# Two of sixteen MLP units by plain products, and their right-hand sums formed later

## The chip, the cores and the metric

The kernel runs on one core of one Trainium2 chip. The metric is device time in microseconds (us) of one execution. Engines are named as the profile names them: PE (TensorE, matmul) with its weight loads PEld, DVE (VectorE), ACT (ScalarE), POOL (GpSimd) and SP, whose queue issues the loads from HBM.

## What is computed

A decoder trunk of two layers on x of 512 tokens by 1024 features, in float32. Each layer is a token mixer, a cross-attention into 256 memory tokens, and an MLP; a norm closes the trunk. The part that matters here:

```
h = h + o.reshape(b, s, 1024) @ w_o                       # end of the cross-attention
n = rmsnorm(h, mlp_norm)                                  # h * rsqrt(mean(h*h) + eps) * gain
h = h + square(relu(n @ w_up)) @ w_down                   # w_up 1024 x 4096, w_down 4096 x 1024
```

The norm's factor per token is not applied to n: h times the gain goes into the matmuls, and the factor's square is multiplied in behind the down projection, since relu and square let it pass (tile Rt).

## The kernel before

Activations lie transposed: hT holds 8 blocks of 128 features by 512 tokens. Float32 accuracy comes from splitting every operand into a rounded high part and a low rest (`hi_lo`: ACT writes the high part, L156 or, with a scale, L159; DVE subtracts it for the low part, L157 or L160), and every product is three matmuls, high by high, high by low, low by high (`mm3`, L177 to L179). Weights are tiles of 128 x 1024: a DMA into a raw tile (tag wr, 2 buffers), then wh and wl (3 buffers each). `chunk` does this for a plain projection, which is 24 matmuls of 512 columns (`proj`).

**The end of the cross-attention** is eight such projections `wo`, one for each block e of hT in the order 0, 4, 1, 5, 2, 6, 3, 7. Behind each, `after_o` adds the result to hT (`add_h`, L474, DVE) and prepares the MLP's right operands; `st.add` squares the block on ACT (L258) and adds it to the tile ssq on POOL (L270).

**The MLP** has four quarters (`qd`). A quarter computes 8 blocks of hidden features, as four units, and then eight plain down projections. A unit (class `Unit`) is a 2 x 2 block scheme with seven products in the place of eight (Winograd's form of Strassen's scheme): its left operands are four quarters of a weight block and four sums of them (A11, A12, A22, S1 to S4), formed by four additions on POOL in `load` (L968); its right operands are 256 columns wide. A product is 12 matmuls of 256 columns, a unit 84. The unit's weights are three raw tiles of 1024 columns (d1, d2, d3) and one of 512 (e, tag ptl).

Right operands: `Right` holds, for a pair of blocks j and j + 4, the quarters B11, B12 (block j, its halves of the tokens), B21, B22 (block j + 4), and T1 = B11 - B12, T2, T3 and Z. Each of B11, T1, B21, B22, T2, T3, Z is split high and low. `first` forms B11 and T1 behind the first block of a pair (the scaled copy at L930, the difference at L932), `second` the others behind the second block (L938 to L943). They stand in the tiles hgh and hgl (B11 with T1, B21 with B22), qkh and qkl (T3, T2) and pth (Z). All four pairs are needed by the first product `0.p1`, since each product sums over the four pairs.

The order of the products in a quarter is a string of names (unit.product) in `mlp`; the tile framework turns program order and priorities into one instruction order per engine, and each engine takes its instructions in that order. `load` and `weight` run at raised priority. In the first quarter `st0.rstd()` (8 matmuls of 2 columns, L292, then L295 on DVE and a power on POOL, L298) stands behind the eighth product and the spread of r2 (L308, Rt) behind the fourteenth.

Of the kernel before, what the change touches and what calls it, by code (L numbers as in the profile page):

```python
# [10 lines left out]
F32R = mybir.dt.float32r  # L11
# [7 lines left out]
D = 1024  # L19
# [17 lines left out]
def build(ctx, tc, a):  # L37
# [125 lines left out]
    def chunk(src):  # L163

        cnt[0] += 1
        i = cnt[0]
        started.append(i)
        with tc.high_priority(100 if len(started) > 4 else 0):
            raw = wp.tile([128, 1024], F32, tag="wr", name=f"wr_{i}", bufs=2)
            h = wp.tile([128, 1024], F32R, tag="wh", name=f"wh_{i}", bufs=3)  # L170
            lo = wp.tile([128, 1024], F32R, tag="wl", name=f"wl_{i}", bufs=3)
            SY.dma_start(out=raw, in_=src)
            hi_lo(h, lo, raw)
        return h, lo

# [721 lines left out]
        return os_, out_steps(3)  # L897

# [8 lines left out]
    class Right:  # L907


        def __init__(self, j, gname, gi):  # L910
            self.j, self.gname, self.gi, self.x = j, gname, gi, {}

        def __getitem__(self, name):
            return self.x[name]

        def tile(self, name):
            cnt[0] += 1
            return wk.tile([128, 1280], F32, tag="p", name=f"{name}_{cnt[0]}", bufs=2)

        def parts(self, names, src, tags):  # L920
            h, lo = t2k(tags[0], F32R), t2k(tags[1], F32R)
            hi_lo(h, lo, src)
            for i, n in enumerate(names):
                self.x[n] = (h[:, i * 256:(i + 1) * 256], lo[:, i * 256:(i + 1) * 256])

        def first(self):

            j = self.j
            self.B = self.tile("B")
            A.activation(out=self.B[:, :1024].rearrange("p (a c) -> p a c", a=4)[:, 0::2, :],  # L930
                         in_=hT[:, j, :].rearrange("p (a c) -> p a c", a=2), func=AF.Copy, scale=col(self.gname, self.gi + j))
            V.tensor_tensor(out=self.B[:, 256:512], in0=self.B[:, 0:256], in1=self.B[:, 512:768], op=ALU.subtract)  # L932
            self.parts(("B11", "T1"), self.B[:, :512], ("hgh", "hgl"))

        def second(self):
            j, B = self.j + 4, self.B
            E = self.tile("E")
            A.activation(out=E[:, :512], in_=hT[:, j, :], func=AF.Copy, scale=col(self.gname, self.gi + j))  # L938
            V.scalar_tensor_tensor(out=E[:, 768:1024], in0=B[:, 256:512], scalar=-1.0, in1=E[:, 256:512],
                                   op0=ALU.mult, op1=ALU.subtract)  # L940
            V.tensor_tensor(out=E[:, 512:768], in0=E[:, 256:512], in1=B[:, 512:768], op=ALU.subtract)
            self.parts(("B21", "B22"), E[:, :512], ("hgh", "hgl"))
            V.scalar_tensor_tensor(out=E[:, 1024:1280], in0=E[:, 768:1024], scalar=-1.0, in1=E[:, 0:256],  # L943
                                   op0=ALU.mult, op1=ALU.subtract)
            self.parts(("T3", "T2"), E[:, 512:1024], ("qkh", "qkl"))
# [84 lines left out]
    def mlp(li, xs, st0, gname, gi, st):  # L1030
        nhg = []

        end = gname is None

        def after_up(qd, i, hid):
            def fn(half, c):
                V.scalar_tensor_tensor(out=c, in0=c, scalar=0.0, in1=c, op0=ALU.max, op1=ALU.mult)
                if end and qd == 3:
                    V.tensor_tensor(out=c, in0=c, in1=Rt, op=ALU.mult)
                h, lo = t2k("acth", F32R), t2k("actl", F32R)  # L1040
                hi_lo(h, lo, c)
                hid[i + 4 * half] = (h, lo)
            return fn

        def after_down(qd, e):
            def fn(ps):
                if end and qd == 3:
                    add_h(e, ps)
                    st.add(e, hT[:, e, :])
                    A.activation(out=hT[:, e, :], in_=hT[:, e, :], func=AF.Copy, scale=col("final_norm", e))  # L1050
                    return
                t = t2k("kv")
                V.tensor_tensor(out=t, in0=ps, in1=Rt, op=ALU.mult)  # L1053
                V.tensor_tensor(out=hT[:, e, :], in0=hT[:, e, :], in1=t, op=ALU.add)
                if qd == 3:
                    new_h(e, gname, gi, nhg, st)
            return fn

        for qd in range(4):
            hid = {}  # L1060
            us = [Unit(a["mlp_up"][li * 16 + qd * 4 + i], xs, after_up(qd, i, hid)) for i in range(4)]
            if qd == 0:

                order = "0.p1 0.p5 1.p1 1.p5 0.p2 0.p6 1.p2 1.p6 0.p7 0.p4 0.p3"
            else:
                order = "0.p1 0.p5 0.p2 0.p6 1.p1 1.p5 0.p7 1.p2 1.p6 0.p4 0.p3"
            order += " 2.p1 2.p5 1.p7 2.p2 2.p6 1.p4 1.p3 3.p1 3.p5 2.p7 3.p2 3.p6 2.p4 2.p3"
            for i, x in enumerate(order.split()):
                getattr(us[int(x[0])], x[2:])()
                if qd == 0 and i == 7:  # L1070
                    st0.rstd()
                if qd == 0 and i == 13:
                    r2 = small(4, tag="r2")
                    V.tensor_tensor(out=r2, in0=st0.r, in1=st0.r, op=ALU.mult)
                    A.activation(out=Rt, in_=spread(r2), func=AF.Copy)
            prev = us[3]
            ks = (0, 4, 1, 5, 2, 6, 3, 7)
            down = [proj(a["mlp_down"][(li * 4 + qd) * 8 + e], hid, after_down(qd, e), ks=ks)
                    for e in range(7 if end and qd == 3 else 8)]
# [167 lines left out]
    for li in range(2):  # L1247
# [35 lines left out]
        wo = [proj(a["xa_w_o"][li * 8 + e], os_, after_o(i, e), need=need) for i, e in enumerate((0, 4, 1, 5, 2, 6, 3, 7))]
        merge(last, [*wo[0][:6], *wo[1][:6]])
        run([*wo[0][6:], *wo[1][6:]])
        for e in range(2, 8):
# [121 lines left out]
```

## Time and profile before

| | |
|---|---|
| runs, median of 3 | 1480.79 us (1480.47 to 1482.84) |
| the profiled execution | 1479.2 us, its span 1477.2 us |
| PE busy | 1425.7 us, 97% of the span |
| DVE, ACT, POOL busy | 1073.5, 747.2, 361.9 us |
| mean granted TensorE clock | 0.991 |
| line of PE over 40 slices | 7999999999899999999999999999998999999996 |

A matmul's record reaches past the start of the next one, because matmuls are pipelined; the time from one start to the next tells what one costs. A bracket at the end of a timeline row gives the idle time of the engine before it and what ended it. The granted clock is 1.00 at 2.4 GHz and 0.50 at 1.2 GHz.

### The profile page before, as it was taken

To read this page: it belongs to the slowest core of one execution; us is meant where nothing else is said; L and a number is where in the kernel's file an instruction comes from. 1 tells how busy PE (TensorE), PEld (TensorE's weight loads), DVE (VectorE), ACT (ScalarE), POOL (GpSimd) and SP (SyncE) were. 2 spreads that over 40 slices of the span, in tenths; PEclk is the share of its full clock that TensorE was granted. 3 is DMA by queue.
4 is the path that set the end of the run, shared out by engine and by line. 5 is a ranking of instruction groups with operands and counts; after the bars stand their busy time and mean duration, and the time that the engine had idled before them with its cause. 6 is when DMAs were issued, how large, how long until landed. Compare 5 with 4: busy or idle time off the path is not lost.

```text
span 1477.2 us, 21427 instructions
## 1 busy us (share of the span) xinstructions
PE 1425.7 (97%) x8064; PEld 1234.2 (84%) x8064; DVE 1073.5 (73%) x1733; ACT 747.2 (51%) x1321; POOL 361.9 (24%) x300
## 2 busy tenths in 40 slices
PE   7999999999899999999999999999998999999996
PEld 5777887888798989889887888788878889898985
DVE  7788876656885867678678989855497667586773
ACT  4777754545452534435457867644354435252452
POOL 3003221002613315051213313200054041422303
PEclk9999999999999999999999999999998999999998
DMA  5222214423132333422332231333222424242221
GB/s 191 83 86 86 73 65 150 136 93 129 50 115 87 117 92 87 134 58 71 110 108 69 79 94 64 100 131 126 100 93 76 125 65 128 72 122 93 72 86 57
DMA packets 55558, 143.03 MB, mean 97 GB/s; under 512 B 6816, under 2 KB 12320, under 8 KB 55456
## 3 DMA queue, kind: packets, MB, share of 16 engines
q1 hardware_dynamic: 54368, 140.63, 30.1%
q8 instruction: 63, 1.03, 0.3%
q10 hardware_dynamic: 1088, 1.05, 0.2%
q14 instruction: 39, 0.32, 0.1%
HBM read 136.15 MB, written 2.10 MB: 94 GB/s over the span
## 4 chain that ended last, share of the span: by engine, by line
PE 75%; DVE 16%; ACT 5%; issue 3%; POOL 0%; DMA 0%; DVEq 0%; ACTq 0%; POOLq 0%
PE mm L177 18%; PE mm L178 18%; PE mm L179 18%; DVE wl L157 4%; PE s L177 3%; PE s L178 2%; PE s L179 2%; PE t L354 2%; PE pv L177 1%; PE pv L178 1%; PE pv L179 1%; ACT wh L156 1%; DVE hT L474 1%; PE mm L233 1%; PE mm L234 1%
## 5 line engine op out<-in xcount | busy, mean ns | idle before, releaser
L156 ACT ACTIVATE wh<-wr 128x1024 fp32r<-128x1024 f32 x214 | 226.1, 1058 | 296.1 <-PE mm L178 224.3
L157 DVE TENSOR_TENSOR wl<-wr,wh 128x1024 fp32r<-128x1024 f32 x214 | 289.0, 1354 | 73.8 <-ACT wh L156 72.1
L177 PE MATMUL mm<-acth,wh 128*128 128x512 f32 (+1 forms) x768 | 299.1, 392 | 0.9 <-DVE hT L474 0.8
L178 PE MATMUL mm<-actl,wh 128*128 128x512 f32 (+1 forms) x768 | 297.9, 388 | 0.1
L179 PE MATMUL mm<-acth,wl 128*128 128x512 f32 (+1 forms) x768 | 297.6, 388 | 0.0
L177 PE MATMUL mm<-hgh,wh 128*128 128x512 f32 (+1 forms) x504 | 188.3, 374 | 7.6 <-ACT hgh L156 6.7
L178 PE MATMUL mm<-hgl,wh 128*128 128x512 f32 (+1 forms) x504 | 185.5, 368 | 4.7 <-DVE hgl L160 3.7
L179 PE MATMUL mm<-hgh,wl 128*128 128x512 f32 (+1 forms) x504 | 184.8, 367 | 0.3
L177 PEld LDWEIGHTS mm<-acth,wh 128*128 128x128 f32 x768 | 144.0, 188 | 30.5 <-ACT acth L156 2.0
L179 PEld LDWEIGHTS mm<-acth,wl 128*128 128x128 f32 x768 | 144.3, 188 | 29.2
L178 PEld LDWEIGHTS mm<-actl,wh 128*128 128x128 f32 x768 | 144.5, 188 | 27.7 <-DVE actl L157 0.7
L270 POOL TENSOR_TENSOR ssq<-ssq,sq 128x512 f32<-128x512 f32 (+1 forms) x48 | 67.2, 1401 | 409.2 <-ACT sq L258 408.8
L348 POOL TENSOR_SCALAR p<-p,den 128x256 f32<-128x256 f32 (+1 forms) x96 | 66.6, 699 | 254.5 <-DVE den L347 190.1
L1053 DVE TENSOR_TENSOR kv<-mm,Rt 128x512 f32<-128x512 f32 x56 | 38.7, 690 | 109.7 <-PE mm L179 109.7
L177 PEld LDWEIGHTS mm<-hgh,wh 128*128 128x128 f32 x504 | 96.5, 191 | 21.9 <-ACT hgh L156 7.1
L968 POOL TENSOR_TENSOR wr<-ptl,d 128x512 f32<-128x512 f32 x32 | 43.9, 1372 | 283.5 <-DVE wl L157 246.3
L178 PEld LDWEIGHTS mm<-hgl,wh 128*128 128x128 f32 x504 | 96.5, 192 | 18.5 <-DVE hgl L160 4.4
L179 PEld LDWEIGHTS mm<-hgh,wl 128*128 128x128 f32 x504 | 96.4, 191 | 14.6 <-DVE wl L157 0.7
L157 DVE TENSOR_TENSOR wl<-d,wh 128x1024 fp32r<-128x1024 f32 x64 | 87.0, 1359 | 22.1 <-ACT wh L156 21.8
L156 ACT ACTIVATE wh<-d 128x1024 fp32r<-128x1024 f32 x64 | 67.4, 1053 | 58.0 <-PE mm L178 42.2
L177 PE MATMUL s<-hgh,wh 128*128 128x256 f32 (+1 forms) x272 | 80.8, 297 | 3.8 <-DVE kv L1008 2.2
L179 PE MATMUL s<-hgh,wl 128*128 128x256 f32 (+1 forms) x272 | 79.7, 293 | 0.0
(322 smaller groups left out, 3297.2 us busy)
## 6 DMA issues: line engine op xcount, KB each, us to landing
wr<-in_mlp_down SPq DMA_DIRECT2D x64, 512.0 KB, 3.3
d<-in_mlp_up SPq DMA_DIRECT2D x64, 256.0 KB, 2.6
wr<-in_cd_w_in SPq DMA_DIRECT2D x18, 512.0 KB, 3.4
wr<-in_xa_q SPq DMA_DIRECT2D x16, 512.0 KB, 3.3
wr<-in_xa_k SPq DMA_DIRECT2D x16, 512.0 KB, 3.3
wr<-in_xa_v SPq DMA_DIRECT2D x16, 512.0 KB, 3.3
wr<-in_xa_w_o SPq DMA_DIRECT2D x16, 512.0 KB, 3.4
ptl<-in_mlp_up SPq DMA_DIRECT2D x32, 256.0 KB, 3.0
```

The costliest lines, as they stand in the source:

```text
L156: A.activation(out=hi, in_=src, func=AF.Copy)
L157: V.tensor_tensor(out=lo, in0=src, in1=hi.bitcast(F32), op=ALU.subtract)
L177: T.matmul(ps, lhsT=wh, rhs=xh, start=start, stop=False, **kw)
L178: T.matmul(ps, lhsT=wh, rhs=xl, start=False, stop=False, **kw)
L179: T.matmul(ps, lhsT=wl, rhs=xh, start=False, stop=stop, **kw)
L233: T.matmul(st["ps"][b], lhsT=xh, rhs=h[:, k2, :], start=k == 0, stop=False)
L234: T.matmul(st["ps"][b], lhsT=xh, rhs=lo[:, k2, :], start=False, stop=False)
L270: eng.tensor_tensor(out=self.ssq, in0=self.ssq, in1=q, op=ALU.add)
L348: G.tensor_scalar(out=p, in0=p, scalar1=dens[:, i:i + 1], scalar2=1.0, op0=ALU.mult, op1=ALU.mult)
L354: T.transpose(ps[:, c:c + 128], src, ident)
L968: G.tensor_tensor(out=out, in0=x, in1=y, op=ALU.add)
L1053: V.tensor_tensor(out=t, in0=ps, in1=Rt, op=ALU.mult)
```

## The change

Units 0 and 1 of the first quarter of each MLP no longer use the seven products. Each is two plain projections of the half of its output (`plain(i, half)`: one weight tile by one DMA of two parts, `chunk`, 24 matmuls of 512 columns, a relu on ACT, then the unit's own `done`). For this, `after_o` splits every block of hT as it is, scaled by the gain (`Right.plain`), into hgh and hgl; the half that held T1 holds B12. The sums T2, T3 and Z of a pair are formed by `sums`, behind the fourth and sixth output projection for pairs 0 and 1, and behind the first and second plain projection for pairs 2 and 3. `t1` writes T1 over B12, after the four plain projections. Units 2 and 3 then run their seven products each, with p5 behind p6 in unit 2's opening. The additions on POOL for units 0 and 1 go.

```
         def plain(self, i):
+            h, lo = t2k("hgh", F32R), t2k("hgl", F32R)
+            hi_lo(h, lo, hT[:, self.j + 4 * i, :], scale=self.g[i])
+            self.x[i] = (h, lo)
+            for k, n in enumerate((("B11", "T1"), ("B21", "B22"))[i]):
+                c = slice(k * 256, k * 256 + 256)
+                self.x[n] = (h[:, c], lo[:, c])
+        def sums(self, D):
+            j, (g1, g2) = self.j, self.g
+            self.d = D[:, j * 256:(j + 1) * 256]
+            V.tensor_tensor(out=self.d, in0=hT[:, j, 0:256], in1=hT[:, j, 256:512], op=ALU.subtract)
             E = self.tile("E")
+            A.activation(out=E[:, :256], in_=hT[:, j + 4, 256:512], func=AF.Copy, scale=g2)
+            V.scalar_tensor_tensor(out=E[:, 256:512], in0=self.d, scalar=g1, in1=E[:, :256], op0=ALU.mult, op1=ALU.add)
+            V.scalar_tensor_tensor(out=E[:, 512:768], in0=hT[:, j, 256:512], scalar=g1, in1=E[:, :256],
                                    op0=ALU.mult, op1=ALU.subtract)
+            V.scalar_tensor_tensor(out=E[:, 768:1024], in0=hT[:, j + 4, 0:256], scalar=g2, in1=E[:, 256:512],
                                    op0=ALU.mult, op1=ALU.subtract)
+            h, lo = t2k("qkh", F32R), t2k("qkl", F32R)
+            hi_lo(h, lo, E[:, 256:768], scale=-1.0)
...
             z = t2k("pth", F32R)
+            hi_lo(z[:, :256], z[:, 256:], E[:, 768:1024], scale=-1.0)
+        def t1(self):
+            hi_lo(*self.x["T1"], self.d, scale=self.g[0])
...
             if qd == 0:
-                order = "0.p1 0.p5 1.p1 1.p5 0.p2 0.p6 1.p2 1.p6 0.p7 0.p4 0.p3"
+                blocks = [xs[k % 4][k // 4] for k in range(8)]
+                def plain(i, half):
+                    def after(ps):
+                        c = t2k("kv")
+                        A.activation(out=c, in_=ps, func=AF.Relu)
+                        us[i].done(half, c)
+                    src = a["mlp_up"][li * 16 + i][2 * half:2 * half + 2].rearrange("a p c -> p a c")
+                    return proj(src, blocks, after, ks=KS)
+                run(plain(0, 0))
+                D = xs[0].d_tile
+                xs[2].sums(D)
+                run(plain(0, 1))
+                xs[3].sums(D)
+                run(plain(1, 0))
+                st0.rstd()
+                run(plain(1, 1))
+                for x in xs:
+                    x.t1()
+                order = "2.p1 2.p2 2.p6 2.p5 3.p1 3.p5 2.p7 3.p2 3.p6 2.p4 2.p3"
...
             def f(ps):
                 add_h(e, ps)
-                if i % 2 == 0:
-                    hg2.append(Right(e, "mlp_norm", li * 8))
-                    hg2[-1].first()
-                else:
-                    hg2[-1].second()
+                if i == 0:
+                    cnt[0] += 1
+                    hg2.extend(Right(j, "mlp_norm", li * 8) for j in range(4))
+                hg2[e % 4].plain(e // 4)
+                if i == 3:
+                    hg2[0].d_tile = hg2[0].tile("D")
+                if i in (3, 5):
+                    hg2[i // 2 - 1].sums(hg2[0].d_tile)
                 st.add(i, hT[:, e, :])
```

Three places of the order that the framework makes of it, in layer 0 (layer 1 has the same moves). The numbers in names count tiles; d_686 and d_698 are raw tiles of units 2 and 3 in the changed kernel.

POOL, from the output projections into the MLP. Before:

```order
L270 TENSOR_TENSOR ssq_3448<-ssq_3448,sq_3_3566 128x512
L968 TENSOR_TENSOR wr_3759<-ptl_3762,d_665_3761 128x512
L968 TENSOR_TENSOR ptl_3762<-ptl_3762,wr_3759 128x512
L968 TENSOR_TENSOR d_665_3760<-wr_3759 128x512
L968 TENSOR_TENSOR d_665_3761<-d_665_3760 128x512
L270 TENSOR_TENSOR ssq_3448<-ssq_3448,sq_4_3608 128x512
```

and now:

```order
L270 TENSOR_TENSOR ssq_3445<-ssq_3445,sq_7_3719 128x512
L971 TENSOR_TENSOR wr_3925<-ptl_3928,d_686_3927 128x512
L971 TENSOR_TENSOR ptl_3928<-ptl_3928,wr_3925 128x512
L971 TENSOR_TENSOR d_686_3926<-wr_3925 128x512
L971 TENSOR_TENSOR d_686_3927<-d_686_3926 128x512
L971 TENSOR_TENSOR wr_4005<-ptl_4008,d_698_4007 128x512
...
L298 TENSOR_TENSOR rstd_3877<-sm_3875,half_neg 128x4
```

The first unit's additions stood behind the fourth addition to ssq, among the output projections; now all eight additions to ssq come first, and the eight additions of units 2 and 3 follow, ahead of the power for rstd.

PE, where the last output projection ends. Before, the first product of unit 0:

```order
L179 MATMUL mm_3704<-acth_3427,wl_3707 128x512
L177 MATMUL mm_3771<-hgh_3444,wh_3776 128x256
L178 MATMUL mm_3771<-hgl_3445,wh_3776 128x256
L179 MATMUL mm_3771<-hgh_3444,wl_3777 128x256
L177 MATMUL mm_3771<-hgh_3511,wh_3776 128x256
```

and now the first plain projection, whose first two blocks are 0 and 4:

```order
L179 MATMUL mm_3683<-acth_3427,wl_3686 128x512
L177 MATMUL mm_3726<-hgh_3441,wh_3728 128x512
L178 MATMUL mm_3726<-hgl_3442,wh_3728 128x512
L179 MATMUL mm_3726<-hgh_3441,wl_3729 128x512
L177 MATMUL mm_3726<-hgh_3454,wh_3728 128x512
```

The width doubles to 512 columns. Block 3, written behind the seventh output projection, was the fourth right operand of the first product; now it is the seventh, and block 7, written behind the last, the eighth.

DVE, from the rstd to the first of unit 3's weights, in the changed kernel:

```order
L295 TENSOR_SCALAR sm_3875<-t_3866 128x4
L1094 TENSOR_TENSOR r_697_4003<-rstd_3877 128x4
L157 TENSOR_TENSOR wl_3961<-d_686_3926,wh_3960 128x1024
L1040 SCALAR_TENSOR_TENSOR kv_3859<-kv_3859 128x512
L160 SCALAR_TENSOR_TENSOR hgl_3442<-D_3536,par,hgh_3441 128x256
L160 SCALAR_TENSOR_TENSOR hgl_3494<-D_3536,par,hgh_3493 128x256
L157 TENSOR_TENSOR actl_3863<-kv_3859,acth_3862 128x512
L160 SCALAR_TENSOR_TENSOR hgl_3586<-D_3536,par,hgh_3585 128x256
L160 SCALAR_TENSOR_TENSOR hgl_3677<-D_3536,par,hgh_3676 128x256
L157 TENSOR_TENSOR wl_4023<-wr_4005,wh_4022 128x1024
```

The weights for 2.p2 (wl_3961, from d2 of unit 2) and the four low parts of T1 for 2.p5 stand behind r_697, which waits for the power on POOL.

## Rows read from the trace of the kernel before

**Rows 1.** The page, the span and part 1: busy time, share, instructions

```profile
span 1477.2 us, 21427 instructions
PE 1425.7 (97%) x8064; PEld 1234.2 (84%) x8064; DVE 1073.5 (73%) x1733; ACT 747.2 (51%) x1321; POOL 361.9 (24%) x300
```

**Rows 2.** Windows (from:to, length, each engine's busy time): projections, opening, down, layer 1's opening

```profile
352.17:382.77 30.60, 30.60 (x137) 25.35 (x135) 29.08 (x31) 17.33 (x28) 20.09 (x13) 1.00 0.26 78
382.77:432.13 49.36, 41.55 (x318) 40.29 (x317) 40.65 (x50) 26.60 (x45) 18.08 (x11) 0.93 0.30 91
432.13:480.00 47.87, 47.87 (x230) 40.18 (x229) 29.41 (x34) 13.60 (x16) 12.62 (x8) 1.00 0.28 88
1105.37:1156.21 50.84, 43.48 (x317) 42.22 (x316) 40.63 (x50) 26.59 (x45) 18.03 (x11) 0.90 0.32 90
```

**Rows 3.** Timeline of PE: where it stood idle, layer 0, then layer 1

```profile
387.36 0.58 PE L177 MATMUL mm<-hgh,wh 128*128 128x256 f32 x1 [3.36 <-ACT hgh L156]
400.87 0.39 PE L177 MATMUL pv<-hgh,wh 128*128 128x256 f32 x1 [2.64 <-DVE kv L1014]
407.51 0.91 PE L308 MATMUL t<-ident,r 128*128 128x128 f32 x6 [0.93 <-DVE r L1074]
...
1109.96 0.56 PE L177 MATMUL mm<-hgh,wh 128*128 128x256 f32 x1 [3.36 <-ACT hgh L156]
1123.47 0.43 PE L177 MATMUL pv<-hgh,wh 128*128 128x256 f32 x1 [2.17 <-DVE kv L1014]
```

**Rows 4.** Windows behind such idle times; the granted clock is the third number from the end

```profile
387.36:393.12 5.76, 5.24 (x23) 4.94 (x24) 5.74 (x8) 3.79 (x6) 2.15 (x3) 0.50 0.35 90
1109.96:1116.78 6.82, 6.28 (x27) 5.99 (x28) 6.64 (x9) 4.85 (x8) 3.19 (x3) 0.50 0.32 80
```

**Rows 5.** Timeline of PE: first and last of 135 and of 34 matmuls in a row

```profile
352.17 0.39 PE L177 MATMUL mm<-acth,wh 128*128 128x512 f32 x1
382.54 0.39 PE L179 MATMUL mm<-acth,wl 128*128 128x512 f32 x1
...
394.00 0.28 PE L179 MATMUL s<-hgh,wl 128*128 128x256 f32 x1
...
397.95 0.28 PE L179 MATMUL mm<-qkh,wl 128*128 128x256 f32 x1
```

**Rows 6.** Timeline of DVE, layer 0

```profile
366.49 1.50 DVE L943 SCALAR_TENSOR_TENSOR E<-E 128x256 f32<-128x256 f32 x1
...
377.02 1.72 DVE L157 TENSOR_TENSOR wl<-wr,wh 128x1024 fp32r<-128x1024 f32 x1
...
383.23 0.41 DVE L943 SCALAR_TENSOR_TENSOR E<-E 128x256 f32<-128x256 f32 x1
...
385.10 1.21 DVE L157 TENSOR_TENSOR wl<-wr,wh 128x1024 fp32r<-128x1024 f32 x1
...
388.34 0.67 DVE L474 TENSOR_TENSOR hT<-hT,mm 128x512 f32<-128x512 f32 x1
```

**Rows 7.** Timeline of POOL: the first and last addition of unit 0, the rstd

```profile
365.98 1.74 POOL L968 TENSOR_TENSOR wr<-ptl,d 128x512 f32<-128x512 f32 x1
...
370.93 1.36 POOL L968 TENSOR_TENSOR d<-d 128x512 f32<-128x512 f32 x1
...
405.08 1.02 POOL L298 TENSOR_TENSOR rstd<-sm,half_neg 128x4 f32<-128x4 f32 x1 [5.15 <-DVE sm L295]
```

**Rows 8.** Timeline of PE: the matmuls of rstd, and the next one

```profile
403.85 0.95 PE L292 MATMUL t<-ones,kv 128*128 128x2 f32 x8
404.67 0.36 PE L177 MATMUL mm<-qkh,wh 128*128 128x256 f32 x1
```

**Rows 9.** Groups by line and form: count, busy, mean ns

```profile
L156 ACT ACTIVATE wh<-d 128x1024 fp32r<-128x1024 f32 x64 | 67.4, 1053 | 58.0 <-PE mm L178 42.2 <-PE s L178 13.0 <-DVE kv L1014 2.3
L160 DVE SCALAR_TENSOR_TENSOR hgl<-hT,par,hgh 128x512 fp32r<-128x512 f32 x32 | 31.8, 1008 | 1.8 <-ACT hgh L159 1.8
```

More of the change, by code (lines that the diff above doesn't have):

```diff
@@ L171, in chunk @@
             lo = wp.tile([128, 1024], F32R, tag="wl", name=f"wl_{i}", bufs=3)
-            SY.dma_start(out=raw, in_=src)
+            SY.dma_start(out=raw if len(src.shape) == 2 else raw.rearrange("p (a c) -> p a c", a=2), in_=src)
             hi_lo(h, lo, raw)
@@ L897, in cross, with plain @@
         return os_, out_steps(3)
+    KS = (0, 4, 1, 5, 2, 6, 3, 7)
     class Right:
         def __init__(self, j, gname, gi):
-            self.j, self.gname, self.gi, self.x = j, gname, gi, {}
+            self.j, self.x = j, {}
+            self.g = [col(gname, gi + j), col(gname, gi + j + 4)]
         def __getitem__(self, name):
             return self.x[name]
+        def plain(self, i):
+            h, lo = t2k("hgh", F32R), t2k("hgl", F32R)
[4 more added lines that the diff above has]
+                self.x[n] = (h[:, c], lo[:, c])
         def tile(self, name):
@@ L918, in tile @@
             return wk.tile([128, 1280], F32, tag="p", name=f"{name}_{cnt[0]}", bufs=2)
[L920 to L933, printed above, removed]
@@ L1061, in mlp @@
             us = [Unit(a["mlp_up"][li * 16 + qd * 4 + i], xs, after_up(qd, i, hid)) for i in range(4)]
+            order = "0.p1 0.p5 0.p2 0.p6 1.p1 1.p5 0.p7 1.p2 1.p6 0.p4 0.p3 2.p1 2.p5 1.p7 2.p2 2.p6 1.p4 1.p3 " \
+                    "3.p1 3.p5 2.p7 3.p2 3.p6 2.p4 2.p3"
             if qd == 0:
-                order = "0.p1 0.p5 1.p1 1.p5 0.p2 0.p6 1.p2 1.p6 0.p7 0.p4 0.p3"
-            else:
-                order = "0.p1 0.p5 0.p2 0.p6 1.p1 1.p5 0.p7 1.p2 1.p6 0.p4 0.p3"
-            order += " 2.p1 2.p5 1.p7 2.p2 2.p6 1.p4 1.p3 3.p1 3.p5 2.p7 3.p2 3.p6 2.p4 2.p3"
+                blocks = [xs[k % 4][k // 4] for k in range(8)]
[17 more added lines that the diff above has]
+                order = "2.p1 2.p2 2.p6 2.p5 3.p1 3.p5 2.p7 3.p2 3.p6 2.p4 2.p3"
             for i, x in enumerate(order.split()):
                 getattr(us[int(x[0])], x[2:])()
-                if qd == 0 and i == 7:
-                    st0.rstd()
-                if qd == 0 and i == 13:
+                if qd == 0 and i == 3:
                     r2 = small(4, tag="r2")
                     V.tensor_tensor(out=r2, in0=st0.r, in1=st0.r, op=ALU.mult)
+                if qd == 0 and i == 8:
                     A.activation(out=Rt, in_=spread(r2), func=AF.Copy)
             prev = us[3]
-            ks = (0, 4, 1, 5, 2, 6, 3, 7)
-            down = [proj(a["mlp_down"][(li * 4 + qd) * 8 + e], hid, after_down(qd, e), ks=ks)
+            down = [proj(a["mlp_down"][(li * 4 + qd) * 8 + e], hid, after_down(qd, e), ks=KS)
                     for e in range(7 if end and qd == 3 else 8)]
@@ L1282, in build @@
         need = [[("xo", k // 2, k % 2)] for k in range(8)]
-        wo = [proj(a["xa_w_o"][li * 8 + e], os_, after_o(i, e), need=need) for i, e in enumerate((0, 4, 1, 5, 2, 6, 3, 7))]
+        wo = [proj(a["xa_w_o"][li * 8 + e], os_, after_o(i, e), need=need) for i, e in enumerate(KS)]
         merge(last, [*wo[0][:6], *wo[1][:6]])
```

11 lines of the change are left out of this document (1 added, 10 removed).

## The prediction

> **What bounds the kernel now.** I read the page first, then windows by stage, then the timelines of PE, DVE and POOL where the stages meet. PE is busy 97% of the span [rows 1], so a change pays only where PE stands idle or runs slowly, or where it does less. The windows show where that is [rows 2]. The output projections of the cross-attention (352.17 to 382.77) and the down projections (from 432.13) have PE busy for their whole length at clock 1.00. Between them lies the MLP's opening, the first 300 matmuls of four units up to the first down matmul: 49.36 us, of which PE is busy 41.55, at a mean clock of 0.93. Layer 1's opening takes 50.84, at 0.90. Those two windows are where the change acts.
>
> What the opening should take comes from the steps between starts [rows 5]: 34 matmuls of 256 columns in a row start 3.95 us apart from first to last, 33 steps of 0.1197 us; 135 of 512 columns take 30.37 us over 134 steps of 0.2267 us. So 300 x 0.1197 = 35.91 us, with 0.82 for the eight matmuls of rstd [rows 8] and 1.21 for the spread of r2 (0.91 for six of its eight records [rows 3]): 37.94 us. Layer 0 loses 49.36 - 37.94 = 11.42 us, layer 1 12.90.
>
> The loss has three idle places [rows 3]. First, PE waits 3.36 us for hgh of block 3, in both layers. Block 3's projection ended 10 us earlier (24 steps before 382.77, at 377.3); what is late is DVE, which adds even the last projection, done at 382.77, to hT only at 388.34 [rows 6]. DVE was busy 29.08 of 30.60 us in the projections [rows 2], and part of that is not its own work: the same subtraction on 256 columns takes 1.50 us at 366.49 and 0.41 at 383.23, and a wl 1.72 against 1.21 [rows 6]. At the slow ones POOL was running additions, from 365.98 to 372.29 those of unit 0 [rows 7]. Second, 2.64 us (2.17 in layer 1) for DVE to take a finished product out of PSUM; third, 0.93 for r2. The rest of the loss is the clock: behind the first wait the granted clock is 0.50, its level of 1.2 GHz, for 5.76 and 6.82 us [rows 4].
>
> **The change, part by part.** *PE's work.* Two units of 168 matmuls at 0.1197 become four plain projections of 96 at 0.2267: 21.76 for 20.11 us, 1.65 us more a layer. The other 132 matmuls (84 of unit 2, 48 of unit 3), rstd and spread stay: 15.80 + 0.82 + 1.21. An opening without waits is then 39.59 us.
>
> The rows price both widths. The Trainium skill, TensorE: Matmul & The Clock Gate, section Back-to-back issue gap, gives a warm gap of N/2.4 + 2.5 ns, 109 ns for 256 columns and 216 for 512, so by an estimate from that page leaving the seven products would cost 2.4 us a layer and not 1.65; it speaks somewhat more against the change. The trace's own steps, 120 and 227, differ from both figures, and the sum goes by them.
>
> *The first wait.* What goes: in the projections, the eight POOL additions of units 0 and 1, and for half of the pairs the sums T2, T3, Z. What comes: a split of each block, ACT at once from hT, and DVE 1.01 us (the same form, [rows 9]). DVE needs per pair of projections 2 x (0.67 add_h + 1.21 wl + 1.01) = 5.8 us, and some 3 more for a pair's sums (six instructions; the three E's have no row, between 0.41 and 1.50 each by the subtraction's two durations; I take 0.41 there, since only ssq's additions run on POOL then). That is below 9 of the 10.9 us that two projections give PE. So DVE should arrive at the end without arrears. Call the end of the last output projection T. Then come add_h, the wl of the third plain chunk (ACT 1.05 ahead of it, [rows 9]), and block 7's low part: T + 3.5 us. The first plain projection needs it as its eighth block, 21 x 0.2267 = 4.8 us after T. Cover 1.3 us, so I cost the step at nothing; without cover each microsecond late is one of PE's. With the wait goes what I put down to it, the 1.2 GHz stretch.
>
> *The second and third wait.* Plain projections have no sums to take out of PSUM in between; the relu on ACT lies beside PE. rstd now stands after the third plain projection, and the spread after 3.p6, far behind r2. Both waits go.
>
> *What is moved into the opening.* POOL's eight additions for units 2 and 3 now begin only when the third plain chunk has left its raw tile and ssq is complete, T + 4 us. One unit takes 6.3 us (365.98 to 372.29 [rows 7]). Unit 3's raw tile is that of the fourth plain chunk, which DVE frees late, at about T + 12 when each addition holds up one of its instructions. So unit 3's additions end at T + 18.3, the power for rstd (1.02 us) at T + 19.5, and DVE, held at r2 until then, does unit 2's wl of d2 by T + 21.4. PE needs it for 2.p2: four plain projections, rstd and 2.p1, 21.76 + 0.82 + 1.44 = T + 24.0. Cover 2.6 us. The four low parts of T1, T + 24 at the latest, are needed by 2.p5 at T + 26.9. T1 itself must wait for the last read of B12, but each pair's block is free after 3, 9, 15 or 21 of the last 24 matmuls. Unit 2's S3 takes the weight buffer that 2.p5 leaves, 2.9 us (24 matmuls) before 2.p7; a tile twice as wide takes 1.05 on ACT and 1.21 to 1.72 on DVE [rows 6, 9], so half of that fits. *SP's queue*: eight part loads become four chunk loads a layer, each issued once its raw tile is free, two projections ahead of use; nothing on the path.
>
> The low parts, sums and relus move DVE's and ACT's load; the four weight tiles of the plain units replace six wide and two narrow ones, so both do less. That has no price on PE.
>
> **The sum.** 49.36 - 39.59 = 9.77 and 50.84 - 39.59 = 11.25: 21.0 us less than the profiled execution's 1479.2, 1458.2. The median of the runs is 1.6 above that execution, so 1459.8 in their terms. I leave 0.35 a layer for small waits of copies that follow each other closely in unit 2 (2.p6 writes the bank of 2.p1 one product later, not two): **1460.5 us**.
>
> **The rivals.** *The sums on POOL hold DVE longer (B).* From the last add_h to the wl of d2 stand 18 DVE instructions, own time about 12.6 us (four wl at 1.21, seven on 512 columns at 0.67 to 1.01, the rest at 0.41 or less). If each of the sixteen with two operands in SBUF waited 1.09 us (1.50 - 0.41), wl would come at T + 30, 6 us late; if only nine do, one for each of POOL's nine additions, it is at T + 22.4 and input waits decide. Between, 3 us late, with a 1.2 GHz stretch of some 6 us (costing 3) behind it, is 6 us a layer: 1459.8 + 12 = 1472. For it: POOL and DVE collided so in rows 6. Against: POOL has no more than nine additions there, and DVE only four projections' light load. The Trainium skill, SBUF — State Buffer, section SBUF: two separate sides, states this as a lock between a DVE instruction with two SBUF inputs and a GpSimd instruction that reads SBUF, held for the whole instruction. By that rule, the trace's 1.50 against 0.41 us agrees.
>
> *Slower (C).* DVE stays as late as before, 5.6 us behind the last projection, because ssq's additions or the new three-operand forms hold it. Then block 7 comes at T + 8.5, not 4.8: PE waits 3.7; the POOL chain starts 5 us later and uses up its cover of 2.6, so 2.4 more; and each of the two waits brings a 1.2 GHz stretch of 5.8 to 6.8 us, some 3 us each. That is 12.1 a layer against the 10.5 that the change gives on average: 1.6 more, twice, 1484. The point from which it decides is a lateness of about 5 us at T. Against: in the projections unit sums on POOL are gone, and DVE's own work is below 9 of each 10.9 us.
>
> *No net change (D).* Waits of about 10 us a layer at other places, or sums that don't come behind the opening at all. The instruction order speaks against the second: ssq first, then units 2 and 3 on POOL.
>
> **How the numbers follow.** Forecast 0.66 (1457.5 to 1464), B 0.20 (1464 to 1477), D 0.04, C 0.05, and 0.05 for more gain than counted, below 1457.5, if work after the opening also starts with less in arrears. About 0.2%, 3 us, is what a measurement of this kernel can tell from no change. Faster by more than that: 0.66 + 0.20 + 0.05 = 0.91; within 0.04; slower 0.05. The range of 1456.5 to 1472 takes in the forecast, its lower neighbour and the nearer half of B, leaving out under 2 in 10.
>
> **What would show it.** Right: the opening, last output matmul to first down matmul, is 39.6 to 41 us in both layers, PE busy throughout at clock 1.00; add_h of block 7 within 1 us of its projection's end; POOL's additions of units 2 and 3 done by T + 20. B: a wait of PE on a wl at 2.p2 or 2.p5, with DVE instructions of 1.5 us and more beside POOL's. C: a wait in the first plain projection on hgh or hgl of block 7. The forecast is wrong if PE is idle over 1 us at once anywhere in the opening, or if the projections ahead of it lose their 100%.

## The result and the profile after

The changed kernel takes 1461.09 us, the median of four runs (1459.64 to 1462.56); the kernel before, run beside it on the same chip, 1481.38 (1480.47 to 1482.84). The ratio is 0.9862, with a 95% interval of 0.9845 to 0.9879: 20.3 us less. The profiled execution of the changed kernel is the fastest of its four, 1459.64 us, with a span of 1457.9; the span is 19.3 us shorter than that of [rows 1].

The page, span and part 1, the rows that answer to [rows 1]:

```profile
span 1457.9 us, 21055 instructions
...
PE 1420.7 (97%) x7920; PEld 1223.3 (84%) x7920; DVE 1051.2 (72%) x1721; ACT 736.9 (51%) x1305; POOL 333.6 (23%) x284
```

PE's share is still 97%, and its busy time only 5 us less. The gain doesn't show in shares, since it lies in two short stretches. These are the windows of the two openings (layer 0, layer 1) and of the projections ahead of the first, which answer to [rows 2]:

```profile
382.75:422.95 40.20, 39.68 (x245) 35.66 (x244) 30.54 (x36) 21.04 (x36) 15.41 (x10) 1.00 0.29 93
1096.76:1136.98 40.22, 39.69 (x246) 35.68 (x244) 30.56 (x36) 21.05 (x36) 15.45 (x10) 1.00 0.30 92
352.20:382.75 30.55, 30.55 (x136) 25.30 (x135) 29.51 (x38) 17.54 (x30) 9.23 (x6) 1.00 0.34 110
```

The openings take 40.20 and 40.22 us where they took 49.36 and 50.84, at clock 1.00 where it was 0.93 and 0.90: 9.16 + 10.62 = 19.78 us. PE has one wait left in each, at 2.p6 (timeline of PE, one row of each layer; the bracket is the idle time and what ended it):

```profile
409.02 0.39 PE L177 MATMUL mm<-qkh,wh 128*128 128x256 f32 x1 [0.52 <-ACT kv L1002]
...
1123.04 0.39 PE L177 MATMUL mm<-qkh,wh 128*128 128x256 f32 x1 [0.54 <-ACT kv L1002]
```

From the first opening's end to the second's start 0.55 us were lost (432.13 to 1105.37 before, 422.95 to 1096.76 now). That is scatter: the later quarters, ahead of their down projections, hold small waits for DVE that differ between executions of one kernel. In layer 0 these parts take 36.53, 36.63 and 36.39 us before, 36.50, 37.38 and 36.24 in this execution, and 36.38, 36.54 and 36.43 in a later one of the same kernel. Three profiles of the changed kernel all have openings of 40.20 to 40.22.

DVE where the stages meet, T = 382.75 being the end of the last output projection (timeline; the rows answer to [rows 6]):

```profile
357.33 0.47 DVE L938 SCALAR_TENSOR_TENSOR E<-D,par,E 128x256 f32<-128x256 f32 x1
...
365.03 1.51 DVE L938 SCALAR_TENSOR_TENSOR E<-D,par,E 128x256 f32<-128x256 f32 x1
...
374.87 1.50 DVE L938 SCALAR_TENSOR_TENSOR E<-D,par,E 128x256 f32<-128x256 f32 x1
...
382.95 0.69 DVE L474 TENSOR_TENSOR hT<-hT,mm 128x512 f32<-128x512 f32 x1 [0.56 <-PE mm L179]
...
384.96 0.74 DVE L160 SCALAR_TENSOR_TENSOR hgl<-hT,par,hgh 128x512 fp32r<-128x512 f32 x1
385.63 1.51 DVE L938 SCALAR_TENSOR_TENSOR E<-D,par,E 128x256 f32<-128x256 f32 x1
...
403.91 0.16 DVE L1094 TENSOR_TENSOR r<-rstd 128x4 f32<-128x4 f32 x1 [2.09 <-POOL rstd L298]
403.99 1.22 DVE L157 TENSOR_TENSOR wl<-d,wh 128x1024 fp32r<-128x1024 f32 x1
405.12 0.68 DVE L1040 SCALAR_TENSOR_TENSOR kv<-kv 128x512 f32<-128x512 f32 x1
```

And POOL, the first and the last addition of units 2 and 3, and the power (these answer to [rows 7]):

```profile
386.82 1.47 POOL L971 TENSOR_TENSOR wr<-ptl,d 128x512 f32<-128x512 f32 x1
...
401.28 1.62 POOL L971 TENSOR_TENSOR d<-d 128x512 f32<-128x512 f32 x1
402.86 1.01 POOL L298 TENSOR_TENSOR rstd<-sm,half_neg 128x4 f32<-128x4 f32 x1
```

The last add_h starts at T + 0.2; before it started 5.6 us behind T. DVE even waits for it, 0.56 us for the product. Block 7's low part ends at 385.70, T + 2.95. POOL's additions end at T + 20.2, DVE stands at r for 2.09 us until the power is done, and the wl that 2.p2 needs is done at 405.21, T + 22.5.

The wait at 2.p6 hangs on the same chain (timeline of ACT; L1002 is the copy of 2.p1's product out of PSUM):

```profile
405.84 0.63 ACT L156 ACTIVATE acth<-kv 128x512 fp32r<-128x512 f32 x1 [2.90 <-DVE kv L1040]
...
408.61 0.36 ACT L1002 ACTIVATE kv<-mm 128x256 f32<-128x256 f32 x1
```

The last matmul of 2.p1 starts at 406.78, the copy only at 408.61. ACT had waited 2.90 us for DVE's kv, which stands behind r and so behind POOL's power, and had four other instructions to do before the copy.

The sums didn't move as the section on the change has it. A pair's sums begin with the E of L938. The four stand at 357.33, 365.03, 374.87 and 385.63: those of three pairs run among the output projections and only the fourth pair's behind T. The program writes pair 2's behind the first plain projection, but the framework's order puts them before T. It was no other way in the kernel before; the third and the fourth pair's sums there (timeline of DVE):

```profile
378.66 1.51 DVE L939 SCALAR_TENSOR_TENSOR E<-B,E 128x256 f32<-128x256 f32 x1
...
390.07 0.41 DVE L939 SCALAR_TENSOR_TENSOR E<-B,E 128x256 f32<-128x256 f32 x1
```

What left the projections is POOL's additions alone. DVE is even a little busier there than before, 29.51 of 30.55 us against 29.08 of 30.60, and gets through 38 instructions in the place of 31: it arrives on time because its instructions are held less, not because there are fewer of them.

### The profile page after: what moved, and what is told of

The parts are those of the page before. It is cut to its first block, busy times and chain, and to the rows that moved or that the text cites. A ratio compares the mean times of both kernels' runs of the same rounds, so it can differ in the third digit from the quotient of the medians.

```text
span 1457.9 us, 21055 instructions
## 1 busy us (share of the span) xinstructions
PE 1420.7 (97%) x7920; PEld 1223.3 (84%) x7920; DVE 1051.2 (72%) x1721; ACT 736.9 (51%) x1305; POOL 333.6 (23%) x284
## 4 chain that ended last, share of the span: by engine, by line
PE 79%; DVE 13%; ACT 4%; issue 2%; POOL 1%; DMA 1%; DVEq 0%; ACTq 0%; POOLq 0%
PE mm L177 20%; PE mm L178 20%; PE mm L179 19%; DVE wl L157 3%; PE s L177 3%; PE s L178 2%; PE s L179 2%; PE t L354 2%; PE pv L178 1%; PE pv L177 1%; PE pv L179 1%; ACT wh L156 1%; PE mm L233 1%; PE mm L234 1%; PE mm L235 1%
## 5 line engine op out<-in xcount | busy, mean ns | idle before, releaser
L177 PE MATMUL mm<-hgh,wh 128*128 128x512 f32 (+1 forms) x552 | 207.3, 376 | 0.9 <-DVE qkl L576 0.7
L178 PE MATMUL mm<-hgl,wh 128*128 128x512 f32 (+1 forms) x552 | 204.4, 370 | 3.6 <-DVE hgl L160 3.6
L179 PE MATMUL mm<-hgh,wl 128*128 128x512 f32 (+1 forms) x552 | 203.9, 369 | 0.0
L178 PEld LDWEIGHTS mm<-hgl,wh 128*128 128x128 f32 x552 | 104.3, 189 | 19.2 <-DVE hgl L160 4.4
L177 PEld LDWEIGHTS mm<-hgh,wh 128*128 128x128 f32 x552 | 104.3, 189 | 17.2 <-DVE qkl L576 1.1
L179 PEld LDWEIGHTS mm<-hgh,wl 128*128 128x128 f32 x552 | 104.1, 189 | 16.4
L157 DVE TENSOR_TENSOR wl<-d,wh 128x1024 fp32r<-128x1024 f32 x56 | 73.9, 1319 | 26.2 <-ACT wh L156 26.2
L156 ACT ACTIVATE wh<-d 128x1024 fp32r<-128x1024 f32 x56 | 59.0, 1054 | 55.3 <-PE mm L178 40.0
L156 ACT ACTIVATE acth<-kv 128x512 fp32r<-128x512 f32 x80 | 50.5, 632 | 64.2 <-DVE kv L1040 50.1
L177 PE MATMUL s<-hgh,wh 128*128 128x256 f32 (+1 forms) x240 | 70.6, 294 | 3.5 <-DVE kv L1011 2.0
```

Of the source, the lines that this page charges most:

```text
L156: A.activation(out=hi, in_=src, func=AF.Copy)
L157: V.tensor_tensor(out=lo, in0=src, in1=hi.bitcast(F32), op=ALU.subtract)
L177: T.matmul(ps, lhsT=wh, rhs=xh, start=start, stop=False, **kw)
L178: T.matmul(ps, lhsT=wh, rhs=xl, start=False, stop=False, **kw)
L179: T.matmul(ps, lhsT=wl, rhs=xh, start=False, stop=stop, **kw)
```

## The experiments

The theory: what the openings lost before came from POOL's additions for the units. Each held back DVE instructions that ran beside it; DVE so came late to the last add_h and to the products, and PE waited and fell to 1.2 GHz. The rivals put it down to DVE's own work (the sums), to the order on POOL, or to the waits inside the opening alone. Ratios are to the kernel before, run beside each.

### Before, without the additions of units 0 and 1

```
-                for out, x, y in ((d1[:, hi], e, d3[:, lo]), ...
+                if self.copy:
+                    for part, dst in ((3, d3[:, hi]), (1, d2[:, hi]), (0, d1[:, hi])):
+                        SY.dma_start(out=dst, in_=self.src[part])
+                for out, x, y in () if self.copy else ((d1[:, hi], e, d3[:, lo]), ...
...
             if qd == 0:
+                us[0].copy = us[1].copy = True
```

> The kernel before, with one part left out: the eight POOL additions of units 0 and 1 in the first quarter of each MLP are not done (three more DMAs a unit fill those tiles, so later shapes and loads stay). Theory, that these additions held DVE up and so made the first wait: the last add_h comes under 2 us after its projection in the place of 5.6, PE's wait for hgh of block 3 falls from 3.36 to under 1 us, the openings fall from 49.4 and 50.8 to 41 to 45 us (the sums of units 2 and 3 still stand in them), in all 1466 to 1473 us. Rival, that DVE's own forms (B, E and their splits) made it late: lateness over 4 us, openings of 47 us or more, in all 1477 us or more.

Measured: 1473.53 us, ratio 0.9947 (0.993 to 0.9964), openings of 46.42 and 45.74. The last add_h is on time and the wait of 3.36 us is gone, but others have grown (timeline of DVE, then of PE, then two windows):

```profile
384.42 0.69 DVE L474 TENSOR_TENSOR hT<-hT,mm 128x512 f32<-128x512 f32 x1 [1.29 <-PE mm L179]
```

```profile
393.79 0.39 PE L178 MATMUL mm<-qkl,wh 128*128 128x256 f32 x1 [1.02 <-DVE qkl L157]
397.21 0.58 PE L177 MATMUL pv<-hgh,wh 128*128 128x256 f32 x1 [2.91 <-DVE kv L1018]
```

```profile
384.22:430.64 46.42, 41.21 (x318) 40.23 (x317) 36.03 (x42) 23.24 (x40) 16.77 (x10) 0.93 0.31 93
397.21:401.00 3.79, 3.79 (x17) 3.79 (x18) 1.50 (x2) 0.00 (x0) 0.00 (x0) 0.50 0.50 138
```

So the unit additions among the projections did cause the first wait. Removing them gains only 3 to 5 us a layer, since the additions of units 2 and 3 stay in the opening and hold DVE there: a wl takes 2.32 us at 389.73 while POOL adds. The total lies just above the theory's upper end, the openings 0.7 to 1.4 us above theirs.

### Before, without any addition in the first quarter

The same flag for all four units.

```
             if qd == 0:
+                for u in us:
+                    u.copy = True
```

> The kernel before, leaving out all sixteen POOL additions of the first quarter of each MLP, those of units 2 and 3 too (three more DMAs a unit fill the tiles). Theory, that the second wait and the 1.2 GHz behind it, which stayed when only the additions of units 0 and 1 went (openings of 46.4 and 45.7 us), come from the additions that then stand in the opening itself: openings of 38 to 41 us, where 37.9 is PE's work, and in all 1459 to 1465 us. Rival, that the four units' own weight splits and sums are too much for DVE there whatever POOL does: openings of 43 us or more, in all 1469 us or more.

Measured: 1457.5 us, ratio 0.9841 (0.9823 to 0.986), below the theory's lower end. The first opening, by its window (the second takes 38.41):

```profile
382.77:421.20 38.43, 38.25 (x317) 37.94 (x316) 28.69 (x42) 23.03 (x40) 2.48 (x2) 1.00 0.44 140
```

And its page, the row that answers to [rows 1]:

```profile
PE 1417.4 (97%) x8064; PEld 1227.8 (84%) x8064; DVE 1046.6 (72%) x1733; ACT 747.0 (51%) x1321; POOL 307.2 (21%) x268
```

With the seven products, their sums T2, T3 and Z on DVE, the old order and the old place of rstd all kept, the opening takes 38.4 us at clock 1.00. DVE has the same 1733 instructions as before and is busy for 26.9 us less. All but 0.5 us a layer of the loss of before hung on these 32 additions, two times 16. The run takes away two things at once, what the additions do to DVE beside them and the waits for their results and for the power queued among them; the next two runs look at the first alone, with work on POOL whose results nobody reads.

### The changed kernel with POOL additions put back

Eight additions a layer to a scratch tile, behind the fourth and fifth projection, where those of units 0 and 1 had stood.

```
                 st.add(i, hT[:, e, :])
+                if i in (3, 4):
+                    scr = cst.tile([128, S], F32, tag="chdm", name=f"scr_{li}_{i}")
+                    for _ in range(4):
+                        G.tensor_tensor(out=scr, in0=hT[:, e, :], in1=hT[:, e, :], op=ALU.add)
```

> The changed kernel with eight additions of 128 x 512 on POOL put among the output projections behind the fourth and fifth (they read hT and write a scratch tile that nobody reads). Theory, that additions there hold DVE up by about 1.1 us each: 8.8 us against some 6 us that DVE has to spare, so the last add_h comes 1 to 4 us after its projection and not 0.2; block 7 is needed only 4.8 us after it, so PE waits 0 to 2.5 us a layer, in all 1461 to 1467 us. Rival, that DVE's own work made it late before: the last add_h is on time, openings of 40.2 us, in all 1460 to 1461.5 us.

Measured: 1470.01 us, ratio 0.9931 (0.991 to 0.9951), openings of 46.15 and 44.72. More than the theory's upper bound; the direction is its own. The theory gave DVE 6 us to spare, where the changed kernel's window among the projections leaves it idle for 1.04 (29.51 busy of 30.55). A group of three additions on POOL, and DVE beside it (two timelines):

```profile
364.26 4.58 POOL L1306 TENSOR_TENSOR scr<-hT 128x512 f32<-128x512 f32 x3 [2.50 <-DVE hT L474]
```

```profile
365.24 1.52 DVE L160 SCALAR_TENSOR_TENSOR hgl<-hT,par,hgh 128x512 fp32r<-128x512 f32 x1
366.68 1.26 DVE L938 SCALAR_TENSOR_TENSOR E<-D,par,E 128x256 f32<-128x256 f32 x1
367.86 1.26 DVE L939 SCALAR_TENSOR_TENSOR E<-hT,par,E 128x256 f32<-128x256 f32 x1
...
376.75 0.67 DVE L474 TENSOR_TENSOR hT<-hT,mm 128x512 f32<-128x512 f32 x1
...
388.66 0.67 DVE L474 TENSOR_TENSOR hT<-hT,mm 128x512 f32<-128x512 f32 x1
```

The first three read two operands from SBUF and take 1.26 to 1.52 us where the changed kernel, away from POOL's additions, shows 0.47 and 0.74; one of POOL's additions takes 1.53 here (4.58 for three). The add_h at 376.75 also stands beside additions, and keeps its 0.67; one of its operands comes from PSUM. The last add_h starts 5.0 us behind its projection. PE then waits in two places (timeline of PE: layer 0, then the last of the short waits and the later one in layer 1; below it windows behind the two places of each layer):

```profile
388.79 0.50 PE L178 MATMUL mm<-hgl,wh 128*128 128x512 f32 x1 [0.70 <-DVE hgl L160]
390.14 0.50 PE L177 MATMUL mm<-hgh,wh 128*128 128x512 f32 x1 [0.62 <-ACT hgh L159]
391.19 0.50 PE L178 MATMUL mm<-hgl,wh 128*128 128x512 f32 x1 [0.54 <-DVE hgl L160]
...
414.48 0.58 PE L177 MATMUL mm<-qkh,wh 128*128 128x256 f32 x1 [2.31 <-ACT kv L1002]
...
1110.54 0.79 PE L178 MATMUL mm<-hgl,wh 128*128 128x512 f32 x1 [0.54 <-DVE hgl L160]
...
1133.78 0.38 PE L177 MATMUL mm<-qkh,wh 128*128 128x256 f32 x1 [0.78 <-ACT kv L1002]
```

```profile
391.70:396.00 4.30, 4.30 (x20) 3.56 (x20) 4.30 (x4) 1.26 (x2) 4.22 (x4) 1.00 0.14 53
414.48:418.48 4.00, 4.00 (x22) 4.00 (x23) 2.60 (x5) 1.53 (x3) 0.00 (x0) 0.61 0.42 135
1110.54:1113.50 2.96, 2.96 (x7) 2.38 (x8) 2.96 (x3) 0.77 (x2) 2.88 (x3) 0.50 0.26 89
1133.78:1137.78 4.00, 4.00 (x33) 4.00 (x34) 2.67 (x5) 2.38 (x4) 0.00 (x0) 1.00 0.39 131
```

These are the two places that rival C named or used: blocks 3 and 7 in the first plain projection, and the chain from POOL's last additions. Both layers have the three short waits of 0.70, 0.62 and 0.54 us; in layer 0 the clock stays at 1.00 behind them and falls behind the second place, in layer 1 it falls to 0.50 behind them and stays at 1.00 behind the second place. The openings are longer than the changed kernel's by 5.95 and 4.50 us, not the 12.1 of that rival.

### The same with fills in the place of additions

```
+                if i in (3, 4):
+                    scr = cst.tile([128, S], F32, tag="chdm", name=f"scr_{li}_{i}")
+                    A.activation(out=scr, in_=hT[:, e, :], func=AF.Copy)
+                    for _ in range(8):
+                        G.memset(scr, 0.0)
```

> The changed kernel, with eight fills of a scratch tile of 512 columns on POOL behind each of the fourth and fifth output projections (sixteen a layer; each group begins with a copy on ACT, which ties it to its projection). A fill writes SBUF and reads nothing, where the additions of e5_pool_back read two operands. Theory: what holds DVE beside POOL is that both read operands from SBUF, so fills cost DVE nothing: openings of 40.2 us as in the changed kernel, the last add_h within 1 us of its projection, DVE's sums E at 0.4 to 0.7 us beside the fills, total 1461 (1459.5 to 1463). Rival: any work of POOL on SBUF holds DVE, or it is the place in POOL's queue that counts (the additions to ssq and those of unit 2 come later): then the last add_h is late by over 2 us, the openings take 42 us or more, and the total is 1465 or more.

Measured: 1460.86 us, ratio 0.9855 (0.9832 to 0.9877), openings of 40.23 and 40.22; the unaltered changed kernel in the same comparison gave 1460.88. POOL, a group of fills and the addition to ssq behind it, and DVE beside both:

```profile
372.59 4.62 POOL L1307 MEMSET scr<- 128x512 f32 x8
377.18 1.76 POOL L270 TENSOR_TENSOR ssq<-ssq,sq 128x512 f32<-128x512 f32 x1
```

```profile
373.72 1.21 DVE L157 TENSOR_TENSOR wl<-wr,wh 128x1024 fp32r<-128x1024 f32 x1
...
375.51 0.48 DVE L938 SCALAR_TENSOR_TENSOR E<-D,par,E 128x256 f32<-128x256 f32 x1
...
377.69 1.52 DVE L160 SCALAR_TENSOR_TENSOR pth<-E,pth 128x256 fp32r<-128x256 f32 x1
```

The fills keep POOL busy for 9.24 us a layer (two groups of 4.62; over the whole span 352.5 us, against 359.4 with the additions and 333.6 in the changed kernel), and its later work queues behind the fills as it did behind them, yet a sum E takes 0.48 us beside fills. A little later, beside the addition to ssq, the pth that takes 0.42 elsewhere takes 1.52. Neither POOL's busy time nor its queue held DVE; additions that read SBUF did.

### Only unit 0 plain

```
                 xs[3].sums(D)
-                run(plain(1, 0))
                 st0.rstd()
-                run(plain(1, 1))
...
-                order = "2.p1 2.p2 2.p6 2.p5 3.p1 3.p5 2.p7 3.p2 3.p6 2.p4 2.p3"
+                order = "1.p1 1.p2 1.p6 1.p5 2.p1 2.p5 1.p7 2.p2 2.p6 1.p4 1.p3 3.p1 3.p5 2.p7 3.p2 3.p6 2.p4 2.p3"
```

> The changed kernel with one plain unit a layer in the place of two; unit 1 goes by the seven products. PE's work falls by 0.82 us a layer. Theory, that the plain projections pay by the time they give DVE and POOL: 10.9 us of cover in the place of 21.8, and unit 1's additions stand among the output projections again, so waits of 1 to 5 us a layer come back: openings of 40.5 to 45 us, in all 1461.5 to 1470 us. Rival, that a single plain unit gives cover enough and the second is a mere price: openings of 39.4 us, in all 1459.5 us. Second rival, that with less than two the waits of before come back whole: openings of 48 us and more, 1477 us.

Measured: 1471.62 us, ratio 0.9937 (0.9921 to 0.9953), openings of 44.63 and 44.61. The openings lie within the theory's range, the total 1.6 us above it. The order of work on POOL moves with it: four unit additions run among the projections again, from 377.58 to 383.63, the last add_h is 3.5 us late, and PE waits in the first plain projection (timeline of PE, the window behind):

```profile
391.76 0.66 PE L178 MATMUL mm<-hgl,wh 128*128 128x512 f32 x1 [2.05 <-DVE hgl L160]
```

```profile
391.76:397.00 5.24, 5.24 (x16) 4.19 (x17) 3.41 (x4) 1.16 (x2) 3.83 (x3) 0.67 0.07 25
```

Half of the change gives half of the gain. What the second plain unit does, by this reading, is to put all unit additions behind the projections and to give DVE light work beside them; the run changes both together and doesn't part them.

### Units 0 and 1 plain in every quarter

```
-            if qd == 0:
+            if True:
                 blocks = [xs[k % 4][k // 4] for k in range(8)]
...
+            if qd == 0:
                 run(plain(0, 0))
...
+            else:
+                for i in range(2):
+                    run(plain(i, 0))
+                    run(plain(i, 1))
+                order = "2.p1 2.p5 2.p2 2.p6 3.p1 3.p5 2.p7 3.p2 3.p6 2.p4 2.p3"
```

> The changed kernel with units 0 and 1 of the other three quarters by plain projections too (there T1 stands in the place of B12, so those results differ). No wait of note stands in the later quarters, so this measures the price of the plain scheme alone, six times. By the steps between starts, 0.2267 and 0.1197 us: 1.65 us each, 9.9 us more than the changed kernel, less up to 3 us of small waits that the seven products have in these quarters: 1468 to 1471 us. By the gap formula of the Trainium skill's page on TensorE (109 and 216 ns): 2.4 us each, 14.2 us more, 1475 us.

Measured: 1465.32 us, ratio 0.9893 (0.9877 to 0.9909); the unaltered changed kernel beside it 1461.6. Six plain quarters cost 3.7 us, not the 7 to 10 expected. A quarter's upward part with plain units, by its window, and two of the changed kernel's, one without a wait (its third profile) and the last quarter (its first profile):

```profile
642.62:680.22 37.60, 37.60 (x230) 33.86 (x229) 22.99 (x24) 16.15 (x25) 13.62 (x8) 1.00 0.19 61
```

```profile
1270.71:1306.70 35.99, 35.99 (x301) 35.98 (x300) 28.98 (x34) 19.84 (x33) 12.71 (x8) 1.00 0.41 119
1354.34:1392.61 38.27, 36.75 (x302) 36.14 (x301) 32.24 (x39) 19.71 (x32) 13.19 (x8) 1.00 0.23 70
```

All six plain quarters take 37.59 or 37.60 us, 225.56 in all; the six of the changed kernel's first profile 221.78. In the quarter of 35.99 us all 300 matmuls start 0.12 us apart, so it holds no wait, and the price against it is 37.59 - 35.99 = 1.60 us. Six of these are 9.6, near the 9.9 expected; but the changed kernel's six quarters lose 221.78 - 6 x 35.99 = 5.8 to waits that the plain ones don't have, more than the 3 that was allowed for them, which leaves 3.8. In the last quarter plain units would even gain 0.7.

### p5 ahead of p6 in unit 2's opening

The left 0.52 us is a wait of 2.p6 for ACT's copy out of the PSUM bank that 2.p1 used. Here 2.p5 goes between.

```
-                order = "2.p1 2.p2 2.p6 2.p5 3.p1 3.p5 2.p7 3.p2 3.p6 2.p4 2.p3"
+                order = "2.p1 2.p2 2.p5 2.p6 3.p1 3.p5 2.p7 3.p2 3.p6 2.p4 2.p3"
```

> The changed kernel with unit 2's opening as p1 p2 p5 p6 in the place of p1 p2 p6 p5. Theory, that the 0.52 and 0.54 us that PE waits at 2.p6 are its bank's copy, for which one product is too short: with two products the wait goes, and the low parts of T1, done 25.3 us after the last output projection, are in time for 2.p5 that now starts at 25.6 us: openings of 39.7 in the place of 40.2 us, in all about 1 us less than the changed kernel. Rival, that a wait for T1 takes its place: openings of 40.2 us or more and a wait of PE on hgh or hgl at 2.p5.

Measured: 1458.89 us, ratio 0.9856 (0.9835 to 0.9877). Two more comparisons set it beside the changed kernel on one chip.

> Unit 2's opening as p1 p2 p5 p6, beside the changed kernel on the same chip. Its openings were 0.8 us shorter each. Theory: 1.6 us less than the changed kernel, a ratio to before lower by 0.001. Rival: what is won in the openings is within what runs differ by, no order between the two.

> The changed kernel once more, beside the next run on the same chip: 1461 us, openings of 40.2 us.

Measured: 1460.66 (0.9859, 0.9843 to 0.9876) against 1461.6 (0.987, 0.9852 to 0.9887).

> e3_p5_first once more, beside the changed kernel on the same chip. The openings should again be 39.4 us against 40.2, 1.6 us less in all; the run times of both have scattered by 3 us, by waits of 0.2 to 1.5 us in the later quarters that differ from one execution to the next. Theory: about 1459.7, 1 to 2 us below the changed kernel. Rival: p5 ahead of p6 moves the wait to another place, and the two are within 0.5 us.

> The changed kernel, unaltered, for comparison with e3c_p5_first on the same chip: 1461.2, openings of 40.2 us with one wait of 0.5 us at 2.p6 in each layer.

Measured: 1459.41 (0.9845, 0.9821 to 0.9869) against 1460.88 (0.9855, 0.9835 to 0.9875). Each pair's intervals overlap, but all six openings of the three profiles are 39.42 or 39.43 us (the window of one):

```profile
382.86:422.28 39.42, 39.42 (x245) 35.62 (x244) 30.55 (x36) 20.99 (x36) 15.39 (x10) 1.00 0.30 95
```

PE is busy for the whole length. The gain of 0.8 us a layer is more than the bracket's 0.52, since the bracket counts from a modelled end: in the changed kernel the waiting matmul at 409.02 starts 0.80 us behind the one before it (408.22), where a step is 0.12, and the one after it 0.23 behind. Over twelve runs each the medians are 1459.7 and 1461.2. The difference of 1.5 agrees with the 1.6 of the windows, but the run times alone, which spread over 4 us and more, don't show it; the windows do. This version has the lowest median of those here that do all the work.

## Why the prediction was right

**The sum.** 1460.5 us was forecast, 1461.09 measured, within the range. An opening without waits was put at 39.59 us; p5 ahead of p6 shows it, 39.42. What was left for the copies at 2.p6, 0.35 a layer, was the right place and too small: the wait costs 0.8. As for its reason, the copies do follow each other closely, but by its timeline ACT came late to the one that 2.p6 needs after it had waited for the end of POOL's chain; no run parts the two. The span fell by 19.3 us where 21.0 less 0.7 was forecast: 19.78 in the openings, less 0.55 of scatter between. That the median came within 0.6 us of the forecast is in part luck, since the four runs lie up to 2.9 us apart.

**The first wait.** As forecast, DVE arrived without arrears and the 1.2 GHz stretch went with the wait. That POOL's additions were behind DVE's lateness was read from one subtraction at 1.50 and 0.41 us; the runs without additions, with additions put back and with fills show it. Two terms of the step were off. For half of the pairs the sums T2, T3 and Z were to leave the projections; none of them did, as the E rows show. And DVE's work, a pair's sums included, was put below 9 of each 10.9 us, some 25 of the window's 30.55; it was busy for 29.51, since beside an addition to ssq the first E of a pair takes 1.50 us and not 0.41, and a split of 512 columns up to 1.78 and not 1.01. So DVE had about 1 us to spare and not 5. The step held because without the unit additions even that was enough.

**Block 7.** Its low part: forecast T + 3.5, measured T + 2.95 against T + 4.8 needed.

**The chain behind the opening.** Of all steps this was the tightest: unit 3's additions forecast to end at T + 18.3, measured T + 20.2, just past the T + 20 that was named as a sign of being right: unit 3's additions take 1.6 to 1.8 us beside DVE's work where unit 2's shortest takes 1.36, and the second one waited 1.06 us for its load; the wl at T + 22.5 against 21.4 forecast, about the 22.4 that rival B gave for nine held instructions; needed at 406.90, T + 24.15. A cover of 2.6 us had become 1.7. The low parts of T1 were done at 408.00, T + 25.3, where T + 24 was the forecast and T + 26.9 the forecast need. On a third path, ACT's copy for 2.p6, which the prediction didn't follow, there was by the timeline no cover, and the 0.8 us are its price. Rival B was nearer than its distance in the total suggests; its wait on a wl didn't occur.

**The price of plain.** 1.65 us a layer was forecast, from the steps of 34 matmuls in a row. Over a whole quarter without waits it is 1.60: 300 matmuls of 256 columns take 35.99 us, 0.1200 each where the 34 gave 0.1197. By an estimate from the figures that the Trainium skill (TensorE: Matmul & The Clock Gate, section Back-to-back issue gap) gives for isolated matmuls it would be 2.4, further off.

**Rival C** was priced too high. At its deciding point, a last add_h 5.0 us late, the added additions gave 1470.01 us, still 11 below the kernel before. In layer 0 the three short waits in the first plain projection delay the matmuls' starts by 2.7 us (1.86 by their brackets), not 3.7. And each layer had one stretch at 1.2 GHz, not two: in layer 0 behind the later wait of 2.31 us, in layer 1 behind the three short ones.

**Still open:** why the small waits in the later quarters differ from one execution to the next, which no run here took apart.

## What to carry to other kernels

When VectorE arrives late at a stage's end, compare the same instruction's duration early and late in the stage before counting its work: here 32 additions on an engine busy a quarter of the time cost 24 us in all (1481.7 against 1457.5). Moving them to a stretch where VectorE has slack is worth some more products on TensorE. A stretch without brackets can still hold a wait: one later quarter took 36.24 us and another 35.99, PE busy throughout in both, and only the steps between starts (two of 0.267 and 0.223 us among 0.12) tell them apart. And where statements of a program are moved, the order that the framework makes of them is to be read before they are counted as moved.

## What was not expected of the hardware

- A fill on POOL of 512 columns takes 0.58 us (eight in 4.62) and leaves DVE alone, where an addition of the same size takes 1.2 to 2.4 and holds DVE instructions with two operands in SBUF. The Trainium skill (SBUF — State Buffer, section SBUF: two separate sides) has DVE with two SBUF inputs blocked only by a GpSimd instruction that reads SBUF; the fills agree with that word.
- The length of a wait alone doesn't tell whether the clock falls behind it. The same three waits of 0.70, 0.62 and 0.54 us were followed by a granted clock of 1.00 in layer 0 and of 0.50 in layer 1. In the kernel before, the window behind the wait of 2.64 us at 400.87 [rows 3] (400.87:405.00) shows 1.00, and behind the shorter one of 2.17 us at 1123.47 it shows 0.53:

```profile
1123.47:1127.00 3.53, 3.53 (x17) 3.53 (x18) 1.50 (x2) 0.00 (x0) 0.00 (x0) 0.53 0.58 149
```

  Behind single waits of 0.52 to 0.60 us it stayed at 1.00 here, and behind 2.05, 2.31, 2.91 and 3.36 it fell (0.67, 0.61, 0.50 and 0.50).
